# The first key and value panels of layer b as a pair in seven products, and one adding transfer cut in halves

## The chip, the cores and the metric

The kernel runs on one core of a Trainium2 chip. The metric is the device time of one execution in microseconds. The engines have these names in the profile: PE (TensorE, matrix products), PEld (its weight loads), DVE (VectorE), ACT (ScalarE), POOL (GpSimd), SP (SyncE, which here only issues transfers).

## The reference, cut to what matters

256 tokens of width 2048 pass a two-layer trunk. Everything is float32.

```python
def sq_relu_mlp(h, g, w1, w2):
    a = jax.nn.relu(rms_norm(h, g) @ w1)          # w1: 2048 x 8192
    return (a * a) @ w2                            # w2: 8192 x 2048
...
    # layer a
    q, k, v, fz = split(rms_norm(h, a_norm_g) @ a_w_in)      # 2048 x (3 * 2048 + 16)
    h = h + forgetting_attention(q, k, v, logf) @ a_w_out
    h = h + sq_relu_mlp(h, ...)
    # keys and values, once, from the stream after layer a
    kv = rms_norm(h, kv_norm_g) @ kv_w                       # 2048 x 4096
    k_sh, v_sh = split(kv)
    # layer b
    q = rms_norm((rms_norm(h, b_norm_g) @ b_w_q), b_q_g)     # 2048 x 2048
    h = h + chunked_relbias_attention(q, k_sh, v_sh, b_rel) @ b_w_out
    h = h + sq_relu_mlp(h, ...)
```

All weights are read once; nearly all the work is the products of 256 tokens with these matrices.

## The kernel before, in words

**Arithmetic.** A float32 product is made of three fast ones. Each weight tile is split into `hi` (ACT, line 318, a rounded copy) and `lo` (DVE, line 319, the rest); each activation tile is split alike. `passes` (lines 585, 587, 589) then gives hi*hi, hi*lo and lo*hi into one PSUM bank.

**Units.** Weights come in units of 128 x 1024 floats (`UN`, 512 KB). A plain unit holds two tiles of 128 rows for one panel of 512 output columns, and `products` makes 12 matrix products of 128 x 128 x 512 of it: two row tiles, two blocks of 128 tokens, three passes. A panel needs 8 plain units.

**Pairs.** Two panels side by side can share their first rows as a `Pair`. Its two token blocks, its even and odd row tiles, and its two panels form a 2 x 2 times 2 x 2 block product, done in seven products in place of eight. The seven right-hand operands are the *forms* `11 T3 T2 T1 21 T4 22`, of the four weight blocks 11, 12, 21, 22: T3 = 22 + 12, T2 = T3 + 11, T1 = 12 + 11, T4 = T2 + 21. An ordinary pair takes two couples of row tiles so (its forms are 1024 wide, 6 matrix products each, in `form_products`), and leaves 6 plain units of each panel (a2 to a7, b2 to b7). A deep pair, in the MLPs, takes four couples (forms 2048 wide, issued as two halves, f and h). Some left-hand operands are sums and differences of activations, made beforehand by `sums` (tiles named S, Sh).

**Who adds.** T3 and T2 are made on DVE (`make`, line 951). T1 and T4 are made by a transfer that adds in flight: `put` (line 960) issues it on POOL's queue, straight from the weights in memory onto the tile of 12 (for T1) or of T2 (for T4). The four blocks are loaded by `bring` (line 925, SP's queue), plain units by `load` (line 294, SP's queue). T2's tile may be overwritten with T4 only when T2 has been split, so `issue` calls `put` for T4 right behind the split of T2's last half:

```python
        if form and form.pair.deep and form.name == "T3":
            make(form.pair, "T2", int(half))
        elif form and half == form.pair.wide:
            ...
            elif form.name == "T2" and form.pair.adds:
                put(form.pair, "T4")
```

**Order.** The whole order of units and forms is a list made before anything is emitted (`plan_heads`, `plan_mlp`, `plan_out`). The last three plain units of a pair (b5, b6, b7) go between the first forms of the next, so every two products of six are followed by one of twelve. `fetch` and `top_up` keep two or three units split ahead of PE, and three more loaded ahead of that. Each engine runs its instructions in the written order. What surrounds the products (norms, transposes, softmax, activation splits) is cut into steps and put into `fill`; `run_fill` emits the next slot after each product. `TABLES` says in which slot each step goes, and, for each pair, how many plain units before its start its blocks 12, 22, 21, 11 are brought and its T3 and T1 are made.

**Transposes by transfer.** Hidden activations are turned by `hop` (line 459): 16 small transfers, alternately on POOL's and SP's queue, named q<-z.

**Around the change.** In layer b, after layer a's MLP, two pairs of query panels (orders "query" and "") are made of `xb`. Then come the keys and values, of `xkv`: the first key panel with its 8 plain units and the first value panel with 5 (`panels`, from `heads_b`), its last three going between the forms of the pair of the second key and value panel; three pairs follow, then two pairs of the output projection, then MLP b. The query pairs end with their own b5, b6, b7, one behind the other. In both MLPs the first block of w1 is an ordinary pair ("early"); the second, with index 1, is the first deep one, of order "ahead1"; later ones alternate "ahead0" and "ahead1" with w2's ("deep0", "deep1").

Of the kernel before, what the change touches and what calls it, by code (L numbers as in the profile page):

```python
# [9 lines left out]
F32 = mybir.dt.float32  # L10
F32R = mybir.dt.float32r
AF = mybir.ActivationFunctionType
ALU = mybir.AluOpType
AX = mybir.AxisListType

P = 128
# [3 lines left out]
KT = D // P  # L20
H = 16
# [6 lines left out]
UN = 1024  # L28
AHEAD = 2
TABLES = {  # L30
    "ATA": ((11, 13, 15, 19, 9), (9, 12, 16, 18, 11), (8, 13, 15, 19, 9), (9, 9, 12, 12, 10)),
    "ATB": ((10, 13, 14, 18, 9), (9, 13, 15, 17, 11), (9, 12, 15, 17, 10), (7, 10, 12, 12, 9)),
# [13 lines left out]
    "LONG": ((0, 1, 2, 5, 9, 10, 11, 14, 14), (0, 0, 0, 4, 7, 9), (1, 0, 1, 2, 5, 5), (1, 0, 1, 4, 5, 5)),  # L46
    "OFH": (11, 10, 1, 7, 7, 7),
    "OFK": (10, 9, 4, 9, 8, 4),
# [3 lines left out]
    "OSH": (7, 9, 7, 5, 5, 1),  # L52
    "OSK": (9, 7, 4, 7, 5, 1),
    "OUTH": "F a2 a3 b2 a4 a5 b3 b4 F G F G b5 a6 a7 G b6 b7 G c2 G c3 G d2 c4 c5 G c6 c7 d3 d4",
    "OUTK": "a2 a3 F b2 a4 F b3 a5 F b4 b5 G G a6 a7 G b6 G c2 b7 d2 G c3 G c4 c5 c6 G c7 d3 d4",
    "QF": (4, 4, 2, 3, 2, 1),
    "QS": (10, 4, 4, 8, 3, 1),
    "RI": (3, 5, 7, 5),
    "SHORT": ((4, 0, 0, 3, 6, 8, 8, 9, 12), (2, 2, 3, 3, 7, 7, 8, 10, 13), (2, 0, 0, 2, 6, 7), (0, 0, 0, 2, 4, 5)),
# [13 lines left out]
    "XOH": (9, 12, 13, 11),  # L73
    "XOK": (9, 14, 12, 14),
    "XS": (0, 5, 6, 2),
}
EARLY = 3
LAZY = ("qkv", "kv", "out0", "out1")
UA = UN // 512
REL = 384  # L80
WIDE = UN + 512
DEEP = 2 * UN
# [16 lines left out]
def trunk(ctx: ExitStack, tc: tile.TileContext, xT, xr, gs, hg, bf, wgate, w_in, w_oa, w1a, w1fa, w1sa, w2fa, w2sa,  # L99
# [48 lines left out]
    units = deque()  # L148
# [45 lines left out]
    def plan_mlp(w1, w1f, w1s, w2f, w2s, rest, when, more=None):  # L194
# [18 lines left out]
        for m, (second, c, q) in enumerate(seq):  # L213
            i = 2 * c + q
            if second:
                add(None, w2f, w2s, i, WIDE2, "deep%d" % q, TABLES["W2L" if i == 7 else "W2S" if q else "W2F"], DEEP)
            else:
                add(w1, w1f, w1s, i, WIDE1, "ahead%d" % q if i else "early", TABLES["W1E" + when] if not i else TABLES["W1I" + when] if i == 1 else TABLES["W1S" if q else "W1F"], DEEP)
            pairs[-1].at = second, c, q
# [4 lines left out]
        plan, rest = join(pairs, rooms, rest)  # L224
        return queue(plan + rest)

# [32 lines left out]

    def plan_heads(w, when, w_out):  # L260
        pairs = []
        for j in range(1, w.shape[0] // 16):
            src = [[w[16 * j + 8 * q + u] for u in range(8)] for q in range(2)]
            big = {k: src[int(k[1]) - 1][int(k[0]) - 1] for k in ("11", "12", "21", "22")}
            pairs.append(Pair(big, src, "qkv" if when == "H" else "kv", j % 2 == 1, TABLES[when + ("F" if j == 1 else "S")]))
            pairs[-1].at = 2 * j
        tail = Tail(w, 8)
        units.extend(w[i] for i in range(13))
        plan, rest = join(pairs, {"12": "k0", "22": "k1", "11": "v0", "21": "v1"}, [(tail, 0, u) for u in range(KT // UA - 3, KT // UA)])
        q = pairs[-1].rooms  # L270
        more, rest = plan_out(w_out, {"12": q["11"], "22": q["12"], "11": q["21"], "21": q["22"]}, rest, when)
        return queue(plan + more), rest, tail

    plan_h, rest, tail_h = plan_heads(w_in, "H", w_oa)
    plan_a = plan_mlp(w1a, w1fa, w1sa, w2fa, w2sa, rest, "H", w_qb)
    plan_k, rest, tail_k = plan_heads(w_kv, "K", w_ob)
    plan_b = plan_mlp(w1b, w1fb, w1sb, w2fb, w2sb, rest, "K")
    ready = deque()

# [20 lines left out]
    def issue(parts=1):  # L300
# [20 lines left out]
        if form and form.pair.deep and form.name == "T3":  # L321
            make(form.pair, "T2", int(half))
        elif form and half == form.pair.wide:
            if form.name == "T3":
                make(form.pair, "T2")
            elif form.name == "T2" and form.pair.adds:
                put(form.pair, "T4")
# [373 lines left out]
    class Rooms:  # L701
# [3 lines left out]
        def open(self):  # L705
            self.t = prob.tile([P, 4 * UN], F32, name="pbuf", tag="p", bufs=1)
            self.n = dict.fromkeys(self.at, 0)

        def __call__(self, name):
            first, n = self.at[name]  # L710
            i = first + self.n[name] % n
            self.n[name] += 1
            return self.t[:, i * 3 * P : (i + 1) * 3 * P]
# [196 lines left out]
    def bring(p, name):  # L910
        if p.order == "out1":
            i = int(name in ("11", "21"))
            if i not in p.box:
                p.box[i] = acts.tile([P, DEEP], F32, name="wB", tag="act")
            p.t[name] = p.box[i][:, name[0] == "2" and UN or 0 :][:, :UN]
        elif p.order in LAZY:
            f, n = owner.get(p.rooms[name], (None, None))
            assert f is None or {"12": "T1", "21": "21", "11": "11", "22": "22"}[n] in f.issued, ("room busy", name, n)
            assert n != "11" or "T2" in f.has
            owner[p.rooms[name]] = p, name  # L920
            p.t[name] = sub(p.rooms[name])[:, UN:]
        else:
            p.t[name] = room(p.rooms[name], "w" + name)
        p.has.add(name)
        SY.dma_start(p.t[name][:, : p.cols], p.big[name])

    def make(p, name, half=None):
# [3 lines left out]
        elif name == "T3":  # L931
            if p.order in ("query", ""):
                t[name] = query_room(0)
            elif p.order in LAZY:
                t[name] = acts.tile([P, 2 * UN], F32, name="wT3", tag="act")[:, :UN]
# [16 lines left out]

    def put(p, name):

# [4 lines left out]
        p.has.add(name)  # L959
        G.dma_start(p.t[name][:, : p.cols], p.big[other], accum_op=ALU.add)  # L960

# [55 lines left out]
    def mlp(plan, x, Sx, st, last, more=None):  # L1017
# [58 lines left out]

        run(plan, open_pair)

# [143 lines left out]
    def heads_b(out):  # L1222
# [19 lines left out]
        evacs = [f(g) for g in range(NG) for f in (of_k, of_v)]  # L1242
        box = [13]

        def after():
            prepare(plan_k[0][0], box[0])
            box[0] -= 1

        panels(xkv, evacs[:1], None, after)
        panels(xkv, evacs[1:2], None, after, tail=tail_k)  # L1250
        base = turns[0]

        last = next(p for p, q, i in plan_k[::-1] if isinstance(p, Pair) and p.order in LAZY[:2])
# [104 lines left out]
```

## Time and profile before

| | |
|---|---|
| time, median of 3 runs | 2059.22 us (2059.14 to 2059.76) |
| time of the profiled execution | 2062.13 us |
| its span, first to last instruction | 2060.3 us |
| PE busy | 2047.3 us, 9068 matrix products |
| DVE busy | 1778.3 us (86%) |
| ACT busy | 1400.0 us (68%) |
| share of the 16 transfer engines, software queue | 22.4% |
| share of the 16 transfer engines, SP's queue | 63.9% |
| granted PE clock, mean | 0.999 |

The profile page gives one execution. Rows of the timeline read: start in us, length in us, engine, line, operation, out<-in, count, and in brackets how long the engine sat idle before it and what ended that. The end of a matrix product is modelled, and products overlap in the pipeline, so lengths of rows overlap; the time that PE needs is read from one start to the next. Rows of waits read: who waited for whom, microseconds in total, times, longest.

### The profile page before, as it was taken

Reading aid. Unit: us, or ns where it says so; the run is one execution under the profiler, and the core shown is the slowest. Engines: PE = TensorE matmul, PEld = TensorE weight load, DVE = VectorE, ACT = ScalarE, POOL = GpSimd, SP = SyncE. Lnnn points to the kernel's source line nnn. Section 1 sums busy time; section 2 is a strip of 40 time slices with the busy share of each in tenths; the row PEclk is TensorE's granted clock in tenths of the full one; section 3 lists DMA queues with packets and bytes.
Section 4 is the critical chain, followed back from the end, with each engine's and each line's share of the span. In section 5 each row is a group of like instructions: output and inputs, shape, how many; then the busy total and the mean of one; then the engine's idle time right before and its main releaser. Section 6 shows DMA issues by size and latency. Waiting matters only on the chain.

```text
span 2060.3 us, 27092 instructions
## 1 busy us (share of the span) xinstructions
PE 2047.3 (99%) x9068; PEld 1690.6 (82%) x9068; DVE 1778.3 (86%) x2058; ACT 1400.0 (68%) x1799; POOL 238.7 (12%) x347
## 2 busy tenths in 40 slices
PE   9999999999999999999999999999999999999999
PEld 8888888878888888888888888888788887888887
DVE  7788798899898899899987778888988988988996
ACT  7766566677677677677788566666766675776764
POOL 1121010011111102101012111001111111111020
PEclk9999999999999999999999999999999999999999
DMA  8898897898888898898878988889988888888985
GB/s 330 258 301 252 275 278 249 292 274 266 293 255 287 267 295 272 248 290 276 252 247 273 288 265 269 251 256 295 279 288 269 266 267 277 262 285 258 293 263 150
DMA packets 174444, 556.72 MB, mean 270 GB/s; under 512 B 40528, under 2 KB 69088, under 8 KB 151264
## 3 DMA queue, kind: packets, MB, share of 16 engines
q1 hardware_dynamic: 153824, 464.99, 63.9%
q0 software_dynamic: 20192, 89.70, 22.4%
q8 instruction: 71, 1.16, 0.2%
q14 instruction: 69, 0.57, 0.1%
q10 hardware_dynamic: 288, 0.30, 0.1%
HBM read 515.02 MB, written 27.29 MB: 263 GB/s over the span
## 4 chain that ended last, share of the span: by engine, by line
PE 88%; DMA 4%; issue 3%; DVE 3%; ACT 1%; SPq 0%; POOL 0%; ACTq 0%; DVEq 0%; POOLq 0%
PE acc L589 21%; PE acc L585 21%; PE acc L587 21%; PE s L585 8%; PE s L587 8%; PE s L589 8%; DVE lo L319 1%; DMA wT<-in_w1fb 1%; DMA q<-turn 1%; PE po L720 1%; PE po L757 1%; DMA w<-in_w2fb 1%; ACT hi L318 1%; DVE z L433 0%; DMA turn<-z 0%
## 5 line engine op out<-in xcount | busy, mean ns | idle before, releaser
L319 DVE TENSOR_TENSOR lo<-raw,hi 128x1024 fp32r<-128x1024 f32 (+1 forms) x414 | 500.3, 1213 | 81.0 <-ACT hi L318 76.6
L318 ACT ACTIVATE hi<-raw 128x1024 fp32r<-128x1024 f32 (+1 forms) x414 | 435.1, 1055 | 195.2 <-PE acc L587 128.6
L585 PE MATMUL acc<-hi,act 128*128 128x512 f32 x1784 | 500.5, 393 | 4.3 <-ACT hi L318 3.7
L589 PE MATMUL acc<-lo,act 128*128 128x512 f32 x1784 | 493.9, 390 | 0.2
L587 PE MATMUL acc<-hi,act 128*128 128x512 f32 x1784 | 493.8, 390 | 0.1
L585 PEld LDWEIGHTS acc<-hi,act 128*128 128x128 f32 x1784 | 333.1, 188 | 75.3 <-ACT hi L318 6.1
L587 PEld LDWEIGHTS acc<-hi,act 128*128 128x128 f32 x1784 | 335.1, 188 | 71.6 <-DVE act L414 1.0
L589 PEld LDWEIGHTS acc<-lo,act 128*128 128x128 f32 x1784 | 334.5, 188 | 72.4 <-DVE lo L319 3.1
L318 ACT ACTIVATE hi<-w 128x1024 fp32r<-128x1024 f32 x258 | 271.4, 1059 | 125.9 <-PE acc L587 83.5
L319 DVE TENSOR_TENSOR lo<-w,hi 128x1024 fp32r<-128x1024 f32 x258 | 310.6, 1219 | 19.6 <-ACT hi L318 17.7
L319 DVE TENSOR_TENSOR lo<-wT,hi 128x1024 fp32r<-128x1024 f32 x220 | 266.9, 1222 | 68.6 <-ACT hi L318 64.7
L318 ACT ACTIVATE hi<-wT 128x1024 fp32r<-128x1024 f32 x220 | 231.8, 1060 | 103.7 <-PE acc L587 42.2
L585 PE MATMUL s<-hi,act 128*128 128x512 f32 x530 | 146.3, 391 | 0.0
L589 PE MATMUL s<-lo,act 128*128 128x512 f32 x530 | 145.0, 389 | 0.4 <-DVE lo L319 0.4
L587 PE MATMUL s<-hi,act 128*128 128x512 f32 x530 | 144.7, 388 | 0.0
L459 POOL DMA_DIRECT2D q<-z x192 | 95.7, 511 | 250.9 <-DVE z L433 214.4
L589 PEld LDWEIGHTS s<-lo,act 128*128 128x128 f32 x530 | 99.2, 188 | 21.4 <-DVE lo L319 1.1
L587 PEld LDWEIGHTS s<-hi,act 128*128 128x128 f32 x530 | 99.4, 188 | 20.6
L585 PEld LDWEIGHTS s<-hi,act 128*128 128x128 f32 x530 | 99.2, 188 | 20.4
L585 PE MATMUL s<-hi,S 128*128 128x512 f32 x288 | 89.6, 392 | 0.0
L587 PE MATMUL s<-hi,S 128*128 128x512 f32 x288 | 88.7, 389 | 0.0
L589 PE MATMUL s<-lo,S 128*128 128x512 f32 x288 | 88.6, 389 | 0.0
(213 smaller groups left out, 2236.3 us busy)
## 6 DMA issues: line engine op xcount, KB each, us to landing
raw<-in_w_in SPq DMA_DIRECT2D x75, 512.0 KB, 5.8
w<-in_w2fa SPq DMA_DIRECT2D x32, 1024.0 KB, 6.2
w<-in_w2fb SPq DMA_DIRECT2D x32, 1024.0 KB, 6.6
w<-in_w1fa SPq DMA_DIRECT2D x28, 1024.0 KB, 7.4
w<-in_w1fb SPq DMA_DIRECT2D x28, 1024.0 KB, 7.1
raw<-in_w2sa SPq DMA_DIRECT2D x52, 512.0 KB, 7.1
raw<-in_w_kv SPq DMA_DIRECT2D x52, 512.0 KB, 5.4
raw<-in_w2sb SPq DMA_DIRECT2D x51, 512.0 KB, 7.6
```

The source lines that it names most:

```text
L318: S.activation(hi[:, c], raw[:, c], AF.Copy)
L319: V.tensor_tensor(lo[:, c], raw[:, c], hi[:, c].bitcast(F32), op=ALU.subtract)
L459: (G if i % 2 else SY).dma_start(dst[32 * j : 32 * j + 32, i * n : (i + 1) * n], z[32 * i : 32 * i + 32, j * n : (j + 1) * n])
L585: TE.matmul(ps[:, cols], xh, cut(hi, j), start=first, stop=False, **kw)
L587: TE.matmul(ps[:, cols], xl, cut(hi, j), start=False, stop=False, **kw)
L589: TE.matmul(ps[:, cols], xh, cut(lo, j), start=False, stop=last, **kw)
L720: TE.matmul(s[:, P : 3 * P], q[:, a, P:T], k[:, a], start=True, stop=True)
L757: TE.matmul(po[:, :T], v[:, 0, a * P : (a + 1) * P], pT[:, :2], start=True, stop=False)
```

## The change

1. The first key and value panels of layer b become an ordinary pair too (order "kv0", table "KZ"): 12 plain units and 7 forms in place of 16 plain units. The calls of `panels` in `heads_b` go. The weights are laid out for it on the host, for all of w_kv.
2. The three last units of the second query pair no longer stand alone at the end of layer a's plan; they go between the first forms of the new pair, and `run` for that plan prepares the new pair's blocks ahead (its argument `follow`).
3. Rooms: the second query pair takes lower halves of the tiles whose upper halves hold the new pair's blocks; the new pair's T3 takes the last quarter of the tile `query`; the softmax tile `pbuf`, which shares a place with `query`, is allotted at its first use and not at the start.
4. In both MLPs the block of w1 with index 1 has order "second" in place of "ahead1" (same list of products). For it, T4's adding transfer is issued in two halves: the left one behind the split of T2's first half, the right one behind that of its second half.
5. Nearly all slots and distances in `TABLES` that belong to the projections, the output projections, the attention and the start of the MLPs are others. Those of the later MLP blocks stay (`T`, `W1F`, `W1S`, `W2F`, `W2S`; `W2L` has one other number).

```diff
-    "KX": ((7, 7, 8, 11, 11), (13, 15), (15, 17), (18, 20)),
+    "KX": ((7, 7, 8, 11, 11), (12, 13), (17, 18), (19, 20)),
+    "KZ": (7, 8, 3, 7, 5, 3),
...
+        "kv": "a2 F a3 a4 F a5 a6 a7 F b2 b3 b4", "qkv": "a2 a3 a4 F a5 F a6 b2 a7 F b3 b4", "kv0": "a2 F a3 a4 F a5 a6 a7 F b2 b3 b4",
...
-    "T0H": ((0, -1, 6, 6, 7, 7, 7, 10, 11), (1, -1, 5, 7, 7, 7, 8, 9, 9), (1, 4, 6, 6, 7, 7), (0, -1, 4, 4, 4, 5)),
-    "T0K": ((0, -1, 5, 5, 6, 6, 6, 7, 10), (1, -1, 5, 5, 6, 6, 7, 8, 8), (1, 3, 6, 7, 7, 7), (0, -1, 4, 4, 4, 4)),
-    "W1EH": (12, 13, 2, 15, 7, 6),
-    "W1EK": (14, 14, 9, 12, 11, 5),
+    "T0H": ((1, -1, 6, 6, 6, 6, 6, 8, 8), (0, -1, 4, 5, 6, 6, 7, 8, 8), (0, 4, 6, 7, 7, 7), (1, -1, 5, 5, 5, 5)),
+    "T0K": ((1, -1, 5, 5, 6, 6, 6, 7, 10), (1, -1, 5, 5, 6, 6, 7, 8, 8), (1, 3, 6, 7, 7, 7), (0, -1, 4, 4, 4, 4)),
+    "W1EH": (14, 15, 2, 10, 7, 6),
+    "W1EK": (13, 14, 7, 12, 12, 4),
     "W1F": (7, 5, 1, 5, 4, 3),
-    "W1IH": (11, 7, 6, 9, 4, 1),
-    "W1IK": (11, 7, 3, 9, 4, 3),
+    "W1IH": (10, 7, 6, 8, 4, 2),
+    "W1IK": (10, 7, 3, 9, 4, 1),
...
-                add(w1, w1f, w1s, i, WIDE1, "ahead%d" % q if i else "early", ...
+                add(w1, w1f, w1s, i, WIDE1, ("second" if i == 1 else "ahead%d" % q) if i else "early", ...
...
-        return queue(plan + rest)
+        return (queue(plan), rest) if more is not None else (queue(plan + rest), [])
...
+        elif form and form.pair.order == "second" and form.name == "T2":
+            put(form.pair, "T4", int(half))
         elif form and half == form.pair.wide:
...
         def open(self):
-            self.t = prob.tile([P, 4 * UN], F32, name="pbuf", tag="p", bufs=1)
+            self.t = None
...
+        elif p.order == "":
+            p.t[name] = sub(p.rooms[name])[:, :UN]
...
+            elif p.order == "kv0":
+                t[name] = query_room(3)
...
-    def put(p, name):
+    def put(p, name, half=None):
...
-        G.dma_start(p.t[name][:, : p.cols], p.big[other], accum_op=ALU.add)
+        cols = slice(0, p.cols) if half is None else slice(half * UN, half * UN + UN)
+        G.dma_start(p.t[name][:, cols], p.big[other][:, cols], accum_op=ALU.add)
...
-        run(plan, open_pair)
+        run(plan, open_pair, None, plan_k[0][0] if more else None)
...
-        panels(xkv, evacs[:1], None, after)
-        panels(xkv, evacs[1:2], None, after, tail=tail_k)
```

More of the change, by code (lines that the diff above doesn't have):

```diff
@@ L30 @@
 TABLES = {
-    "ATA": ((11, 13, 15, 19, 9), (9, 12, 16, 18, 11), (8, 13, 15, 19, 9), (9, 9, 12, 12, 10)),
-    "ATB": ((10, 13, 14, 18, 9), (9, 13, 15, 17, 11), (9, 12, 15, 17, 10), (7, 10, 12, 12, 9)),
[1 row of a table removed]
+    "ATA": ((10, 13, 15, 19, 9), (9, 12, 15, 18, 12), (8, 13, 15, 19, 9), (9, 9, 12, 12, 10)),
+    "ATB": ((11, 12, 14, 18, 9), (9, 13, 15, 17, 11), (9, 12, 15, 17, 10), (7, 10, 12, 12, 10)),
[1 row of a table added]
     "GS": (1,),
[11 rows of a table removed]
-    "LONG": ((0, 1, 2, 5, 9, 10, 11, 14, 14), (0, 0, 0, 4, 7, 9), (1, 0, 1, 2, 5, 5), (1, 0, 1, 4, 5, 5)),
-    "OFH": (11, 10, 1, 7, 7, 7),
-    "OFK": (10, 9, 4, 9, 8, 4),
[3 rows of a table removed]
-    "OSH": (7, 9, 7, 5, 5, 1),
[12 rows of a table added]
+    "LONG": ((0, 1, 2, 5, 9, 10, 11, 14, 14), (0, 0, 0, 4, 7, 9), (0, 0, 1, 2, 5, 5), (1, 0, 1, 4, 5, 5)),
+    "OFH": (11, 10, 2, 7, 7, 6),
+    "OFK": (9, 9, 4, 8, 8, 4),
[3 rows of a table added]
+    "OSH": (10, 7, 9, 6, 5, 1),
     "OSK": (9, 7, 4, 7, 5, 1),
[L54 to L57, printed above, removed]
+    "OUTH": "F a2 a3 a4 b2 a5 b3 b4 F F G G b5 a6 a7 G b6 b7 G c2 G c3 G d2 c4 c5 c6 G c7 d3 d4",
+    "OUTK": "a2 a3 F b2 a4 F b3 a5 F b4 b5 G G a6 a7 G b6 G c2 b7 G d2 c3 G c4 c5 c6 G c7 d3 d4",
+    "QF": (4, 3, 2, 4, 2, 1),
+    "QS": (10, 4, 4, 8, 4, 2),
     "RI": (3, 5, 7, 5),
-    "SHORT": ((4, 0, 0, 3, 6, 8, 8, 9, 12), (2, 2, 3, 3, 7, 7, 8, 10, 13), (2, 0, 0, 2, 6, 7), (0, 0, 0, 2, 4, 5)),
[1 row of a table removed]
+    "SHORT": ((4, 0, 0, 4, 7, 7, 7, 8, 11), (2, 2, 3, 3, 7, 7, 8, 11, 13), (4, 0, 0, 2, 6, 6), (0, 0, 1, 2, 4, 5)),
[1 row of a table added]
     "T": ((1, -1, 5, 14, 14, 14, 15, 20, 20), (0, 2, 8, 10, 10, 14, 18, 20, 22), (0, -1, 5, 6, 7, 7), (0, -1, 4, 5, 5, 5)),
[4 rows of a table removed]
[4 rows of a table added]
     "W1F": (7, 5, 1, 5, 4, 3),
[2 rows of a table removed]
[2 rows of a table added]
     "W1S": (8, 6, 4, 5, 4, 1),
     "W2F": (6, 5, 1, 5, 4, 3),
[1 row of a table removed]
[1 row of a table added]
     "W2S": (7, 7, 4, 5, 3, 1),
-    "XOH": (9, 12, 13, 11),
-    "XOK": (9, 14, 12, 14),
-    "XS": (0, 5, 6, 2),
+    "XOH": (9, 13, 12, 11),
+    "XOK": (10, 14, 12, 14),
+    "XS": (0, 5, 5, 0),
 }
 EARLY = 3
-LAZY = ("qkv", "kv", "out0", "out1")
+LAZY = ("qkv", "kv", "kv0", "out0", "out1")
 UA = UN // 512
@@ L217, in plan_mlp @@
             else:
-                add(w1, w1f, w1s, i, WIDE1, "ahead%d" % q if i else "early", TABLES["W1E" + when] if not i else TABLES["W1I" + when] if i == 1 else TABLES["W1S" if q else "W1F"], DEEP)
+                add(w1, w1f, w1s, i, WIDE1, ("second" if i == 1 else "ahead%d" % q) if i else "early", TABLES["W1E" + when] if not i else TABLES["W1I" + when] if i == 1 else TABLES["W1S" if q else "W1F"], DEEP)
             pairs[-1].at = second, c, q
@@ L258, in plan_out, with plan_heads @@
         return plan, [(b, 1, u) for u in (5, 6, 7)]
-    def plan_heads(w, when, w_out):
+    def plan_heads(w, when, w_out, rest=None):
         pairs = []
-        for j in range(1, w.shape[0] // 16):
+        for j in range(1 if rest is None else 0, w.shape[0] // 16):
             src = [[w[16 * j + 8 * q + u] for u in range(8)] for q in range(2)]
             big = {k: src[int(k[1]) - 1][int(k[0]) - 1] for k in ("11", "12", "21", "22")}
-            pairs.append(Pair(big, src, "qkv" if when == "H" else "kv", j % 2 == 1, TABLES[when + ("F" if j == 1 else "S")]))
+            order = "qkv" if when == "H" else "kv" if j else "kv0"
+            pairs.append(Pair(big, src, order, j % 2 == 1, TABLES["KZ" if j == 0 else when + ("F" if j == 1 else "S")]))
             pairs[-1].at = 2 * j
-        tail = Tail(w, 8)
-        units.extend(w[i] for i in range(13))
-        plan, rest = join(pairs, {"12": "k0", "22": "k1", "11": "v0", "21": "v1"}, [(tail, 0, u) for u in range(KT // UA - 3, KT // UA)])
+        tail = None
+        if rest is None:
+            tail = Tail(w, 8)
+            units.extend(w[i] for i in range(13))
+            rest = [(tail, 0, u) for u in range(KT // UA - 3, KT // UA)]
+        plan, rest = join(pairs, {"12": "k0", "22": "k1", "11": "v0", "21": "v1"}, rest)
         q = pairs[-1].rooms
@@ L274, in trunk @@
     plan_h, rest, tail_h = plan_heads(w_in, "H", w_oa)
-    plan_a = plan_mlp(w1a, w1fa, w1sa, w2fa, w2sa, rest, "H", w_qb)
-    plan_k, rest, tail_k = plan_heads(w_kv, "K", w_ob)
-    plan_b = plan_mlp(w1b, w1fb, w1sb, w2fb, w2sb, rest, "K")
+    plan_a, rest = plan_mlp(w1a, w1fa, w1sa, w2fa, w2sa, rest, "H", w_qb)
+    plan_k, rest, _ = plan_heads(w_kv, "K", w_ob, rest)
+    plan_b, rest = plan_mlp(w1b, w1fb, w1sb, w2fb, w2sb, rest, "K")
     ready = deque()
@@ L705, in open @@
         def open(self):
-            self.t = prob.tile([P, 4 * UN], F32, name="pbuf", tag="p", bufs=1)
+            self.t = None
             self.n = dict.fromkeys(self.at, 0)
         def __call__(self, name):
+            if self.t is None:
+                self.t = prob.tile([P, 4 * UN], F32, name="pbuf", tag="p", bufs=1)
             first, n = self.at[name]
@@ L1242, in heads_b @@
         evacs = [f(g) for g in range(NG) for f in (of_k, of_v)]
[L1243 to L1247, printed above, removed]
-        panels(xkv, evacs[:1], None, after)
-        panels(xkv, evacs[1:2], None, after, tail=tail_k)
         base = turns[0]
@@ L1335 @@
         "w2sa": m2[0][2],
-        "w_kv": np.concatenate([_cols_a(kv[:, :1024]), _cols_a(kv[:, 1024:], True)]),
+        "w_kv": _cols_a(kv, True),
         "w_qb": _cols_a(i["b_w_q"][0], True),
```

31 rows, old and new, of the table TABLES are left out of this document.

## The prediction

> **What bounds the kernel now.** I read the page first, then the waits, then PE's own timeline for the places where its products do not follow one another without a gap.
>
> ```profile
> span 2060.3 us, 27092 instructions
> PE 2047.3 (99%) x9068; PEld 1690.6 (82%) x9068; DVE 1778.3 (86%) x2058; ACT 1400.0 (68%) x1799; POOL 238.7 (12%) x347
> ```
>
> PE is busy for 2047.3 of 2060.3 us. So an edit can help in two ways only: fewer matrix products, or fewer of the few microseconds in which PE stands or runs slowly. The change tries both. Where PE stands is told by the waits (who, for whom: us, times, longest) and by PE's timeline around the block of w1 with index 1, in layer a and in layer b:
>
> ```profile
> ACT hi L318 <- DMA wT<-in_w1fb: 12.8, 7, 3.8
> ACT hi L318 <- DMA wT<-in_w1fa: 8.6, 4, 3.2
> ```
>
> ```profile
> 433.36 0.61 PE L589 MATMUL acc<-lo,act 128*128 128x512 f32 x2
> 435.20 0.73 PE L585 MATMUL acc<-hi,act 128*128 128x512 f32 x2 [1.23 <-ACT hi L318]
> 437.95 0.62 PE L589 MATMUL acc<-lo,act 128*128 128x512 f32 x2
> 438.41 1.08 PE L585 MATMUL acc<-hi,act 128*128 128x512 f32 x4
> ...
> 1453.16 0.73 PE L589 MATMUL acc<-lo,act 128*128 128x512 f32 x2
> 1455.61 1.09 PE L585 MATMUL acc<-hi,act 128*128 128x512 f32 x2 [1.71 <-ACT hi L318]
> 1459.59 0.62 PE L589 MATMUL acc<-lo,act 128*128 128x512 f32 x2
> 1460.06 1.08 PE L585 MATMUL acc<-hi,act 128*128 128x512 f32 x4
> ```
>
> What a product costs is read from plain units (x4 per pass, three passes) and from forms (x2 per pass), at the old panels' start and at the first form behind them:
>
> ```profile
> 1118.19 1.07 PE L585 MATMUL acc<-hi,act 128*128 128x512 f32 x4
> 1120.91 1.07 PE L585 MATMUL acc<-hi,act 128*128 128x512 f32 x4
> ...
> 1153.55 0.61 PE L585 MATMUL s<-hi,act 128*128 128x512 f32 x2
> 1154.91 1.07 PE L585 MATMUL acc<-hi,act 128*128 128x512 f32 x4
> ```
>
> A plain unit takes 1120.91 - 1118.19 = 2.72 us, a form of six 1154.91 - 1153.55 = 1.36 us, a pass of two 0.45 us.
>
> **Part 1: seven products in place of eight.** Sixteen plain units took 16 x 2.72 = 43.52 us of PE; 12 units and 7 forms take 12 x 2.72 + 7 x 1.36 = 42.16 us. That is 6 products of 9068, **1.36 us** less, and it lies wholly on the path, since PE is the path. The stretch has no gap to win besides:
>
> ```profile
> 1030.00:1050.00 20.00, 19.59 (x87) 15.91 (x86) 18.45 (x20) 16.11 (x26) 1.13 (x2) 1.00 0.84 271
> ...
> 1090.00:1110.00 20.00, 20.00 (x90) 16.57 (x89) 14.23 (x16) 17.38 (x31) 3.08 (x2) 1.00 0.73 218
> 1110.00:1130.00 20.00, 20.00 (x90) 16.53 (x89) 14.57 (x17) 14.30 (x25) 5.34 (x6) 1.00 0.94 294
> 1130.00:1150.00 20.00, 20.00 (x90) 16.57 (x89) 13.28 (x15) 12.62 (x23) 3.61 (x3) 1.00 1.00 337
> ```
>
> The columns are the stretch, its length, then busy us of PE, PEld, DVE, ACT, POOL, then granted clock, share of the transfer engines, GB/s. What the pair adds beside PE comes from these groups (busy us, mean ns):
>
> ```profile
> L319 DVE TENSOR_TENSOR lo<-raw,hi 128x1024 fp32r<-128x1024 f32 (+1 forms) x414 | 500.3, 1213 | 81.0 <-ACT hi L318 76.6
> L318 ACT ACTIVATE hi<-raw 128x1024 fp32r<-128x1024 f32 (+1 forms) x414 | 435.1, 1055 | 195.2 <-PE acc L587 128.6
> L951 DVE TENSOR_TENSOR wT<-wT,w 128x1024 f32<-128x1024 f32 x62 | 76.0, 1225 | 2.1
> L990 DVE SCALAR_TENSOR_TENSOR acc<-s,p 128x512 f32<-128x512 f32 x24 | 16.6, 692 | 0.9 <-PE s L589 0.9
> L985 ACT ACTIVATE p<-s 128x512 f32<-128x512 f32 x24 | 14.4, 598 | 31.4 <-PE s L589 31.4
> ```
>
> DVE gets three more splits, T3 and T2, and two combinations of accumulators: 3 x 1.21 + 2 x 1.23 + 2 x 0.69 = 7.5 us. ACT gets three splits and three copies of an accumulator: 3 x 1.06 + 3 x 0.60 = 5.0 us. The pair starts where the query pair's b5 started, near 1110, and lasts with those three units 42.16 + 8.16 = 50 us. In 1110 to 1150 DVE has 40 - 27.85 = 12.2 us free and ACT 40 - 26.92 = 13.1 us, so both fit on the whole, and DVE would come to nearly 18 of 20. Locally it is tighter: between the first forms two units need 2 x 1.06 us of ACT in 4.08 us of PE instead of 1.06 in 2.72. The nearest stretch that did stall, 1030 to 1050, had DVE at 18.45 and ACT at 16.11 of 20 and lost 0.41 us of PE. Bounds: nothing, or several such losses, 2 us; below nothing it cannot go, as 1090 to 1150 has no idle PE. I take **+0.6**, by that row.
>
> T1 and T4 of the new pair are two more issues on POOL, and 1 MB more on the software queue. Adding transfers of this size in the other key and value pairs show:
>
> ```profile
> L960 POOL DMA_DIRECT2D R<-in_w_kv x3: 853/860/902, 1148.9 to 1226.6; - x3
> DMA to landing us min/median/max: 5.3/6.3/9.1
> ```
>
> T4 has, from T2's product to its own, b7, T1, a2, 21, a3, a4: 4 x 2.72 + 2 x 1.36 = 13.6 us against 9.1 at worst; T1 has three plain units and then 11, b5, T3, b6, T2, b7, over 20 us, less the two or three units that splitting runs ahead. Both are covered; were they not, the stall would be the excess. POOL is busy for 3 to 5 of 20 us there; the query norms' small operations queued behind a `put` that waits for DVE stand there too; ACT scales by their result, and the cover is the two or three split units ahead of PE, 5 to 8 us. The blocks' loads on SP come about 15 us earlier than the units they replace, where the transfer engines have room (0.73 against 1.00 later).
>
> **Part 2: T4 in halves.** The 1 MB adding transfer is issued when T2's second half is split; the tile is due when T4's product comes up.
>
> ```profile
> 418.57 2.55 DVE L319 TENSOR_TENSOR lo<-wT,hi 128x1024 fp32r<-128x1024 f32 x2
> ...
> 1438.32 2.54 DVE L319 TENSOR_TENSOR lo<-wT,hi 128x1024 fp32r<-128x1024 f32 x2
> ```
>
> ```profile
> 421.69 0.93 POOL L960 DMA_DIRECT2D wT<-in_w1fa  x1 [3.74 <-DVE lo L319]
> ...
> 1441.43 0.95 POOL L960 DMA_DIRECT2D wT<-in_w1fb  x1 [2.72 <-DVE lo L319]
> 1446.74 3.47 POOL L459 DMA_DIRECT2D q<-z  x7 [4.37 <-DVE z L433]
> ```
>
> ```profile
> 434.09 2.01 ACT L318 ACTIVATE hi<-wT 128x1024 fp32r<-128x1024 f32 x2 [2.34 <-DMA wT<-in_w1fa]
> ...
> 1454.50 2.00 ACT L318 ACTIVATE hi<-wT 128x1024 fp32r<-128x1024 f32 x2 [1.85 <-DMA wT<-in_w1fb]
> ```
>
> In layer b it takes until ACT's start about 13.1 us (1441.43 to 1454.50), in layer a 12.4 (421.69 to 434.09), and in both ACT, then PE, wait for it. The loss in layer a: PE was due at 433.36 + 0.45 = 433.81 and starts at 435.20, 1.39 us; the two halves of T4 then take until 438.41, 3.21 us in place of 2 x 1.36 = 2.72. Together 1.9. In layer b: due 1453.61, starts 1455.61, 2.0 us; the two halves last until 1460.06, 4.45 in place of 2.72, 1.7 more. Together 3.7. The 1.7 are the clock:
>
> ```profile
> 1455.60:1459.30 3.70, 3.69 (x9) 2.95 (x10) 3.70 (x4) 2.91 (x3) 0.00 (x0) 0.54 0.85 322
> ```
>
> The granted clock (0.54) is lost for 3.7 us right behind the stall: 3.7 x 0.46 = 1.7. Not every stall of that length does it; a later one, in w2, runs at 0.45 us a pass straight afterwards:
>
> ```profile
> 1733.90 1.07 PE L589 MATMUL s<-lo,act 128*128 128x512 f32 x4
> 1736.90 0.70 PE L585 MATMUL acc<-hi,Sh 128*128 128x512 f32 x2 [1.93 <-DVE acc L990]
> 1737.43 0.62 PE L587 MATMUL acc<-hi,Sh 128*128 128x512 f32 x2
> ```
>
> The Trainium skill, "TensorE: Matmul & The Clock Gate", section Part 1, puts the drop behind an idle window of about 3.4 us of a free-running monitor, so by its rule this stall would cost only its own 2.0 us and part 2 could win 1.7 less; the row of granted clock decides here, since a stall of 2.0 us was followed by it.
>
> With halves, the left one can go once T2's first half is split, about 1.3 us earlier (half of the x2 rows: 1439.6 in b, 419.8 in a). If the transfer as a whole does not end any sooner, the right half still lands at 434.1 and 1454.5, but it is due one form, 1.36 us, later, and the left half is long there. The right half's hi is then done 1.06 us after its landing: 435.15 against 435.17 due in a, 1455.5 against 1454.97 due in b; its lo, 1.22 us later, is due two passes, 0.91 us, after hi. Left over: 0.3 in a, 0.9 in b. So part 2 wins 5.6 at most, if the right half comes earlier too, and 5.6 - 1.2 = 4.4 if it doesn't, and I take the middle, **5.0**. In b the drop of the clock goes with the stall. The added issue (0.95 us on POOL) stands ahead of q<-z's part on POOL, which begins 4 us later, and so delays nothing. Next late after it is nothing of T4; the next gap of PE is the one at 1736.90, which this edit does not touch.
>
> **Part 3: the other slots.** The products of layer a, and their count, stay; only the steps beside them move. PE's gaps there that a slot can move are, beside those above, of half a microsecond each; I take 0, and 2 us either way.
>
> **Sum.** On the profiled execution: -1.36 + 0.6 - 5.0 = -5.8, so 2062.13 - 5.8 = 2056.3, and a span near 2054.5. That execution is 2.91 us above the median of the timed runs. Whatever the timed runs do not have of it may be in these very stalls, so I let a third of the 2.91 off the gain: 4.8 us, and 2059.22 - 4.8 = **2054.4**.
>
> **Rivals.**
>
> *The halves arrive too late.* Two transfers of 512 KB could go one after the other, each with its own start and landing. At the median and the maximum of the rows of that size: left half 1439.6 + 6.3 = 1445.9, right half 1445.9 + 9.1 = 1455.0, which in a is 419.8 + 15.4 = 435.2. Then T4's second half is 1.1 and 1.1 late in hi, 1.4 with lo, and in b the clock is lost again (1.7): 4.5 of the 5.6 remain. Time 2059.22 - 1.36 - 1.1 + 0.6 = 2057.4. For it: the same 16 engines serve SP's loads, and the whole transfer needs up to 13 us though its median is less:
>
> ```profile
> DMA to landing us min/median/max: 8.0/10.5/13.0
> ```
>
> Against it: halves overlap, and 6.3 is far below 10.5. The Trainium skill, "DMA: Bandwidth & Descriptors", section Bandwidth, speaks for it: batch to 1 MiB and more, as each transfer has a fixed cost of about 2.0 us; by that the right half would land 2 us later. If the splits wait for both halves, so that the change does not do what it says, the time is the same. Chance 0.2.
>
> *The stalls were mostly the profiled execution's.* If the timed runs lack all 2.91 us of them, part 2 wins 2.1: 2059.22 - 1.36 - 2.1 + 0.6 = 2056.4. For it: the gap between the two times. Against: the transfer's lateness repeats in both layers. Chance 0.2.
>
> *Slower: ACT becomes the bound where the new pair starts.* ACT has 17.38 of 20 us busy in 1090 to 1110, of which splitting weights is
>
> ```profile
> 1090.00:1110.00 20.00, 7.84 (x8) 1.00 0.73 218
> ```
>
> so 9.5 us are other steps, mostly the activations of the keys and values, and these move into slots 17 to 20, towards the new forms. Four forms and three units last 13.6 us and need 7 x 1.06 = 7.4 of ACT; 6.2 are left. If all 9.5 fall there, 3.3 us are late, with a drop of the clock 5.0; it decides against the gain as soon as the lateness is over 5 us, for instance when it meets the query norms' wait behind POOL twice (2 x 5.0 = 10.0 with clock): 2059.22 + 10.0 - 1.36 - 4.0 = 2063.9. Against it: in 1110 to 1130 ACT has 5.7 us free. Chance 0.1.
>
> **How the numbers follow.** The forecast has 0.5. About 0.2%, 4.1 us here, is what a measurement of this kernel can tell from no change; faster by more is below 2055.1. My forecast lies 0.7 below that line. Of its 0.5, 0.43 falls below, and of the second rival's 0.2, which lies 1.3 above the line, 0.07 (part 3 can move either by 2 us): faster 0.5. Slower, above 2063.3, has the third rival: 0.1. Same has the first rival and what is left of the others: 0.4. The range goes from 2059.22 - 1.36 - 5.6 - 2 = 2050.3 (every stall of part 2, and part 3's 2 us) to 2059.22 - 1.36 + 0.6 + 2 = 2060.5 (nothing of part 2, and part 3 against it). Outside are the rest of the third rival, and half of the cases beyond either end, 2 in 10.
>
> **What would show it.** In the changed profile: 9062 products; two issues of wT<-in_w1fa and wT<-in_w1fb about 1.3 us apart for index 1, ACT no longer idle on them, no wait of PE there, granted clock 1.00 behind it; 7 forms and 12 units where the panels were, PE at 20.00 of 20 in the stretches from 1090 to 1160, DVE near 18. I am wrong if PE waits for hi or lo in that stretch, if the right half of T4 lands over 1.4 us later than the whole did, or if gaps of PE come up in layer a.

## The result, and the profile after

The changed kernel takes 2055.39 us (median of 14 runs, 2053.08 to 2059.78); the kernel before, on the same chip, 2059.18 us (14 runs, 2056.45 to 2061.5). The ratio is 0.998, 95% interval 0.9973 to 0.9987, so 2.7 to 5.6 us less. The profiled execution took 2053.61 us. Its page, where it answers to the lines shown of before:

```profile
span 2051.8 us, 27095 instructions
PE 2042.6 (100%) x9062; PEld 1688.9 (82%) x9062; DVE 1784.1 (87%) x2065; ACT 1404.8 (68%) x1805; POOL 244.2 (12%) x351
```

The two profiled spans differ by 8.5 us, the medians by 3.8: executions of one kernel differ by several microseconds, among other things because a transfer lands a little sooner or later in front of a wait (layer b's T4 below). So I don't compare spans below. Outside the new pair and a few units of the output projections, PE makes the same products in the same order in the kernels of this table, so a stretch of its work is timed from the start of one product to the start of another (numbered as in the kernel before), and a difference is thereby put in its place. Later runs are in this table too; their edits follow. "T4 whole" and "T4 in halves" say how T4's transfer is issued for the w1 block with index 1.

```
us of PE between two products, one execution each (us = start in the kernel before)
                  T4 whole                                               T4 in halves
stretch     us    before before_2 b_slots_a a_pair a_whole a_s5whole | b_halves after after_2 a_late a_t0h a_slot5 a_best
1620- 1900  364   64.45  63.50    64.09     64.91  66.72   63.54     | 63.48    63.47 64.97   63.50  65.83 63.72   64.41
1900- 2600  428  161.81 161.73   162.42    161.79 161.83  161.01     |161.95   161.31 161.51 161.05 161.25 160.07 161.81
4640- 4760 1054   26.99  26.99    26.99     27.17  27.45   27.46     | 27.25    28.17 27.95   28.16  27.95 28.10   26.99
4760- 5080 1081   72.53  72.53    72.53     71.17  71.17   71.89     | 72.53    71.17 71.17   71.17  71.17 71.17   71.17
6260- 6450 1414   47.30  43.94    45.19     44.58  46.09   44.19     | 43.65    43.65 43.89   43.65  43.65 43.69   43.67
7000- 7800 1586  183.53 181.37   181.35    181.35 181.36  183.69     |181.36   181.37 181.93  181.36 181.35 182.45 181.39
8500- 9067 1928  128.16 128.33   128.29    127.38 127.37  127.37     |128.23   127.36 127.37  127.37 127.37 127.38 127.36
```

4760-5080 holds the first key and value panels; 6260-6450 holds T4 of layer b's w1 block with index 1; 1900-2600 that of layer a; 4640-4760 the query pairs. Names that begin with b are the kernel before with an edit, with a the changed kernel with one; the new pair is in the a-kernels and in after. Below, PE's *excess* at a place is what PE loses there against its even pace of 0.227 us a product, gaps over 0.2 us counted.

**Layer b's T4.** PE's, POOL's and ACT's timelines of the changed kernel, at the place where PE stood for 2.0 us and then ran at half clock:

```profile
1450.13 0.61 PE L594 MATMUL acc<-hi,act 128*128 128x512 f32 x2
1450.65 0.74 PE L596 MATMUL acc<-lo,act 128*128 128x512 f32 x2
1451.23 0.64 PE L592 MATMUL acc<-hi,act 128*128 128x512 f32 x2
...
1452.39 0.73 PE L596 MATMUL acc<-lo,act 128*128 128x512 f32 x2
...
1454.34 1.07 PE L592 MATMUL acc<-hi,act 128*128 128x512 f32 x4
```

```profile
1436.48 0.92 POOL L974 DMA_DIRECT2D wT<-in_w1fb  x1 [1.80 <-issue]
1438.66 0.86 POOL L974 DMA_DIRECT2D wT<-in_w1fb  x1 [1.26 <-DVE lo L324]
```

```profile
1448.83 1.30 ACT L402 ACTIVATE Sh<-sum 128x512 fp32r<-128x512 f32 x2 [1.51 <-DVE sum L396]
1450.04 1.99 ACT L323 ACTIVATE hi<-wT 128x1024 fp32r<-128x1024 f32 x2
```

```profile
1455.00:1460.00 5.00, 5.00 (x23) 4.13 (x22) 5.00 (x6) 3.77 (x5) 0.00 (x0) 1.00 0.99 406
```

Two issues, 2.2 us apart. ACT goes from its Sh step straight to T4's two halves and waits for no transfer, passes follow at 0.45 to 0.7 us, and the granted clock is 1.00 (the last row; columns as in the prediction's rows of this kind).

**Layer a's T4.** Here PE stands as long as before, but for another engine:

```profile
431.83 0.61 PE L594 MATMUL acc<-hi,act 128*128 128x512 f32 x2
433.80 0.72 PE L596 MATMUL acc<-lo,act 128*128 128x512 f32 x2 [1.35 <-DVE lo L324]
```

```profile
430.74 1.04 ACT L323 ACTIVATE hi<-wT 128x1024 fp32r<-128x1024 f32 x1
432.13 1.06 ACT L323 ACTIVATE hi<-wT 128x1024 fp32r<-128x1024 f32 x1 [0.35 <-DMA wT<-in_w1fa]
```

```profile
429.92 1.23 DVE L1048 TENSOR_TENSOR act<-q,act 128x1024 fp32r<-128x1024 f32 x1 [1.91 <-ACT q L1044]
431.06 0.42 DVE L395 TENSOR_TENSOR sum<-q 128x256 f32<-128x256 f32 x1
...
432.53 1.22 DVE L324 TENSOR_TENSOR lo<-w,hi 128x1024 fp32r<-128x1024 f32 x1
```

T4 is there in time (the ACT rows). But DVE stood 1.91 us for ACT's step of the first hidden block, then made that block's low part and its sums, and only at 432.53 the lo that PE wanted from 432.28. It is the lo of the block in front of T4 (w, not wT), wanted one pass before T4. It is done at 433.75, and PE goes on at 433.80.

**The queries.** The one place that became slower. The waits around T3 of the second query pair:

```profile
DVE query L964 <- DMA R<-in_w_qb: 2.6, 1, 2.6
```

```profile
PE s L596 <- DVE lo L324: 0.7, 1, 0.7
```

DVE stands 2.6 us for a block that was asked for only then, and a split behind it reaches PE late.

**The new pair itself.** The stretches, columns as before:

```profile
1090.00:1110.00 20.00, 20.00 (x90) 16.57 (x89) 16.52 (x18) 17.53 (x33) 6.51 (x4) 1.00 1.04 330
1110.00:1130.00 20.00, 20.00 (x90) 16.53 (x89) 17.75 (x21) 16.58 (x26) 5.74 (x5) 1.00 1.00 303
1130.00:1150.00 20.00, 20.00 (x90) 16.57 (x89) 12.59 (x14) 12.00 (x22) 3.60 (x3) 1.00 0.90 264
```

PE stays at 20.00 of 20; in 1110 to 1130 DVE rises from 14.57 to 17.75 and ACT from 14.30 to 16.58, under what the stretch holds.

### The profile page after: what moved, and what is told of

It is laid out like the page before. It is cut to its first block, busy times and chain, and to the rows that moved or that the text cites. A ratio compares the mean times of both kernels' runs of the same rounds, so it can differ in the third digit from the quotient of the medians.

```text
span 2051.8 us, 27095 instructions
## 1 busy us (share of the span) xinstructions
PE 2042.6 (100%) x9062; PEld 1688.9 (82%) x9062; DVE 1784.1 (87%) x2065; ACT 1404.8 (68%) x1805; POOL 244.2 (12%) x351
## 4 chain that ended last, share of the span: by engine, by line
PE 94%; DVE 3%; DMA 1%; ACT 1%; issue 1%; SPq 0%; ACTq 0%; POOL 0%; DVEq 0%; POOLq 0%
PE acc L596 22%; PE acc L592 22%; PE acc L594 22%; PE s L596 9%; PE s L592 9%; PE s L594 9%; DVE lo L324 1%; DMA raw<-in_w_in 1%; PE po L729 1%; PE po L766 1%; ACT hi L323 0%; PE po L767 0%; PE po L728 0%; DMA turn<-z 0%; DMA raw<-in_w_qb 0%
## 5 line engine op out<-in xcount | busy, mean ns | idle before, releaser
L324 DVE TENSOR_TENSOR lo<-raw,hi 128x1024 fp32r<-128x1024 f32 (+1 forms) x409 | 494.1, 1212 | 80.4 <-ACT hi L323 76.3
L323 ACT ACTIVATE hi<-raw 128x1024 fp32r<-128x1024 f32 (+1 forms) x409 | 429.7, 1054 | 192.2 <-PE acc L594 131.0
L323 ACT ACTIVATE hi<-w 128x1024 fp32r<-128x1024 f32 x254 | 267.1, 1058 | 127.9 <-PE acc L594 85.2
L324 DVE TENSOR_TENSOR lo<-w,hi 128x1024 fp32r<-128x1024 f32 x254 | 305.5, 1218 | 15.3 <-ACT hi L323 13.5
```

The lines of the kernel that those rows point to most:

```text
L323: S.activation(hi[:, c], raw[:, c], AF.Copy)
L324: V.tensor_tensor(lo[:, c], raw[:, c], hi[:, c].bitcast(F32), op=ALU.subtract)
```

## The experiments

The main theory is called late transfer: the gain beside the 1.36 us of the pair is that T4 no longer comes after its product is due. The rival is that the moved slots give it.

**Halves alone** (b_halves), on the kernel before (cut: the block with index 1 also takes the order "second", and `put` its argument `half`, as in the change):

```diff
+        elif form and form.pair.order == "second" and form.name == "T2":
+            put(form.pair, "T4", int(half))
```

> The kernel before with one edit: T4 of the w1 block with index 1 in halves; no new pair, all slots as before. Theory 'late transfer' (T4's 1 MB comes after its product is due, halves cure that): in layer b the stall at T4 and the clock's drop behind it go, 3.0 to 3.7 us of the profiled span; in layer a 1.6 to 1.9 us; over many runs 2 to 5 us below before (ratio 0.9976 to 0.999). Theory 'other slots' (the gain of the whole change comes from the steps that moved, in layer a and at the queries): within 1 us of before, and ACT still waits on wT. PE products 9068.

Measured: ratio 0.9998, interval 0.9987 to 1.0008, so 2.7 us less to 1.6 us more. Layer b's stretch was 43.65 us, as short as in any kernel, as expected; layer a's 161.95 us, no gain. PE waits near 433 all the same (its waits between 425 and 440: sum, count, longest in us):

```profile
PE acc L591 <- DVE lo L319: 1.6, 1, 1.6
```

That lo is T4's own. DVE made it behind the first hidden block's work, as it did in the kernel before, where the wait for the transfer covered it; DVE's timeline of the kernel before:

```profile
432.58 1.22 DVE L1034 TENSOR_TENSOR act<-q,act 128x1024 fp32r<-128x1024 f32 x1
433.71 0.42 DVE L388 TENSOR_TENSOR sum<-q 128x256 f32<-128x256 f32 x1
...
435.19 2.36 DVE L319 TENSOR_TENSOR lo<-wT,hi 128x1024 fp32r<-128x1024 f32 x2
```

The right half of T4 was late besides, as ACT's timeline of b_halves shows:

```profile
435.69 1.06 ACT L318 ACTIVATE hi<-wT 128x1024 fp32r<-128x1024 f32 x1 [2.58 <-DMA wT<-in_w1fa]
```

Its hi is done at 436.75, 1.5 us after the 435.28 at which PE would have wanted it. The forecast of 2 to 5 us is not borne out over the runs.

**The change without halves** (a_whole): the same two lines taken out of the changed kernel.

> The changed kernel with T4 of index 1 whole again; the new pair and its slots stay. 'Late transfer': PE waits for hi of wT in layer b again, 1.5 to 2.2 us, with or without a drop of the clock of 1.7 us, and in layer a about 1.4 us, partly hidden there by the other stall that the changed kernel has at that place; time 1 to 4 us above the changed kernel, that is within 2 us of before. 'Other slots': as the changed kernel, 2055.4, ratio 0.998. PE products 9062.

Measured: 2058.42 us, ratio 0.9983 (0.9973 to 0.9992). Layer b's stretch is 46.09 us, with 1.8 us of excess. The wait for T4's hi is back, but it is 0.7 of the 1.8; 0.9 is a wait one pass earlier, for the lo of the block in front of T4. Most of the gain over before is there without halves: 3.5 us by the ratio, of 5.4 in a_late (next), on the same chip.

**Both halves written behind T2's second half** (a_late):

```diff
-            put(form.pair, "T4", int(half))
+            if half:
+                put(form.pair, "T4", 0)
+                put(form.pair, "T4", 1)
```

> The changed kernel, with both halves of T4 issued one behind the other after the split of T2's second half, so cut in two but not earlier. If the later due time of the right half is what helps: at most 0.6 us more stall per layer than the changed kernel, time within 1 us of it. If the earlier issue of the left half helps (1.3 to 2.2 us earlier): the left half lands late, PE waits 1 us or more for its hi in layer b, with the clock dropping up to 1.7 more, time 1 to 3 us above the changed kernel.

Measured: 2055.69 us, ratio 0.9974 (0.9963 to 0.9984), layer b's stretch 43.65 us. On the same chip the mean of its 7 runs is 2.6 us below that of a_whole's 11 (interval by resampling the runs, 1.1 to 4.1), so with the pair and its slots halves do gain time. It does not tell the two cases apart, since the issues stand where they stood:

```profile
1436.53 0.92 POOL L976 DMA_DIRECT2D wT<-in_w1fb  x1 [1.52 <-issue]
1438.71 0.86 POOL L976 DMA_DIRECT2D wT<-in_w1fb  x1 [1.25 <-DVE lo L324]
```

In the changed kernel they are at 1436.48 and 1438.66. POOL is idle there and goes as soon as the left half's own split is done, wherever the issue is written. So this is the changed kernel once more.

The transfer's packets say more on the two cases in layer b. Counted from the time at which T4's product was due by PE's even pace, the whole transfer's last packet came 0.2 to 1.5 us ahead in the six executions with T4 whole. In the seven with halves the right half's last packet came 0.5 to 1.8 us ahead and the left half's 4.3 to 5.8. So the whole hardly ends sooner in halves. ACT begins on the left half 1.0 us ahead of due, over 3 us after its last packet, and its issue is earlier by 1.8 to 2.2 us only, so the left half does not need that. This points to the due times: the left half is long there, and the right half is due a form later. A run with the issue alone moved was not made; b_due below moves the due time alone.

**The slots of layer a alone** (b_slots_a): the kernel before with the changed kernel's tables for layer a.

> The kernel before, with the changed kernel's table entries for layer a alone (its projections, attention, output projection and MLP start: ATA, HF, HM, HS, OFH, OSH, OUTH, SHORT, T0H, W1EH, W1IH, XOH, XS); no new pair, T4 whole. Theory 'slots of layer a' (the moved steps there are worth the microseconds that halves alone did not give): 1.5 to 3 us below before, ratio near 0.9988. Theory 'pair and its slots': within 1 us of before.

Measured: 2058.81 us, ratio 0.9994 (0.9985 to 1.0004): 1.2 us less, not clear of none.

**The pair and layer b's slots alone** (a_pair): the changed kernel with layer a's tables of before and T4 whole.

> The changed kernel with T4 of index 1 whole and the table entries of layer a as before: what is left of the change is the new pair and the slots of layer b. By the count of products alone 1.36 us below before, ratio 0.9993. Theory 'pair and its slots': 3 us or more below before, ratio at or under 0.9985. Theory 'slots of layer a': 1 to 2 us below.

Measured: 2058.0 us, ratio 0.9984 (0.9975 to 0.9993): 3.3 us less, more than the products' 1.36. The key and value stretch is 71.17 instead of 72.53 us, 1.36 to the digit. The last stretch is 127.38 instead of 128.13 to 128.33 in the kernel before and all its variants; the difference lies wholly at T4 of the last w1 block, where ACT waits 1.5 us for the transfer in a_pair (none in the changed kernel) and PE not at all, against ACT's 3.8 us before:

```profile
ACT hi L318 <- DMA wT<-in_w1fb: 3.8, 1, 3.8
```

So 0.9 us come from the slots at the end of layer b. Of the tables for these last blocks only one number of `W2L` differs (block 21 is brought one unit earlier), so it is the likely entry; it was not tried alone.

**The kernel before once more** (before_2):

> The kernel before once more, for its profile. If the stalls at T4 belong to the kernel: PE waits 1.3 us or more near 433 and near 1453 again. If they belonged to one execution: at most one of the two shows. The 2.1 us near 1735 should not return, if it was an accident of that execution.

Measured: 2056.07 us, 6.06 less than its first profiled execution, with the same program. Near 433 PE's excess is 1.6 us again. In layer b the wait is nearly gone in this execution, and the 2.1 us near 1735 are gone too (181.37):

```profile
ACT hi L318 <- DMA wT<-in_w1fb: 0.2, 1, 0.2
```

So T4's lateness in layer b belongs to the kernel, but its size to the execution: 43.94 to 47.30 us in six executions with T4 whole, mean 45.21, against 43.65 to 43.89 in seven with halves, mean 43.69. Halves are worth 1.5 us there (1.4 without a_whole's 0.9 us for another block), not the 3.7 of the one profile; among the profiles the drop of the clock occurs in that one alone.

**Later due, T4 whole** (b_due), on the kernel before (cut: the block with index 1 also takes the order "second"):

```diff
-        "second": "a4 F F a5 a6 a7 F b4"},
+        "second": "a4 F a5 F a6 a7 F b4"},
```

> The kernel before with T4 whole, but in the w1 block with index 1 the product with T4 comes one plain unit (2.72 us) later: list a4 F a5 F a6 a7 F b4 in place of a4 F F a5 a6 a7 F b4. Theory 'late by its due time': in layer b the T4 stretch falls to 43.7 to 44.0 us, as with halves, from 43.9 to 47.3 with T4 whole (mean of five 45.2); time 0.5 to 3 us below before. Rival (another wait takes its place): the stretch stays at 44.5 or more.

Measured: layer b's stretch 43.89 us, as expected; but the time is 2063.82 us, ratio 1.0006 (0.9993 to 1.0018). The next stretch (6450-7000) takes 127.57 instead of about 125.04, with waits for lo like this:

```profile
1472.71 1.20 PE L589 MATMUL s<-lo,act 128*128 128x512 f32 x4 [0.76 <-DVE lo L319]
```

The wait for the transfer goes with the later due time alone, and waits for lo come in its place; what makes these late was not followed.

**Layer a's slots, first try** (a_t0h): `T0H[0]` from `(1, -1, 6, 6, 6, 6, 6, 8, 8)` to `(1, -1, 6, 6, 7, 7, 7, 10, 11)`.

> The changed kernel with one table entry of layer a other: the steps of the first hidden block of MLP a after its transpose in slots 6 6 7 7 7 10 11, as before, in place of 6 6 6 6 6 8 8. Theory: the 1.5 us in which PE waits for a lo near 433 come from three ACT steps and a DVE step of that block set into one slot ahead of a unit's split; then that stall goes and layer a wins 1.2 to 1.8 us against the changed kernel, time about 2054. Rival (the right half of T4 is what is late in layer a, and takes the stall's place): PE still waits 1 us or more there, for hi of wT.

Measured: 2057.02 us, ratio 0.9977 (0.9969 to 0.9985). PE's excess near 433 stays at 1.7 us, for lo and not for hi: T4's own lo, made at 437.42 behind the hidden block's sums, as in b_halves. My slots were wrong, and so was the rival.

**Second try** (a_slot5): `T0H[0] = (1, -1, 5, 5, 6, 6, 6, 7, 10)`, as layer b has it.

> The changed kernel with the steps of MLP a's first hidden block in slots 5 5 6 6 6 7 10, those that layer b has, in place of 6 6 6 6 6 8 8. Theory: layer a's 1.5 us wait near 433 comes from that block's DVE steps standing in front of a split, since its transpose is used one slot later than in layer b; then the wait falls to 0.3 or less, as in layer b, and the time is 1.0 to 1.8 us below the changed kernel, ratio to before 0.997 to 0.9975. Rival (the transpose lands too late for slot 5): ACT then waits for q<-z ahead of the splits, and PE's wait stays at 1.5 us or grows.

Measured: 2056.67 us, ratio 0.9979 (0.997 to 0.9988). The excess near 433 is 0.23 us, the stretch 160.07, the shortest of all; the gain in time is below what the runs can tell.

**The same with T4 whole** (a_s5whole):

> The changed kernel with the slots 5 5 6 6 6 7 10 in layer a, and T4 whole. Theory 'two covers in layer a' (the late transfer and the hidden block's steps each make PE wait there, and taking away one leaves the other): PE waits 1 us or more again near 433, now for hi of wT, and the stretch is 161.3 to 161.9 us, against 160.1 with both cures. Rival (the slots alone were the cause): it stays near 160.1. In layer b the T4 stretch is 44 us or more.

Measured: 2059.12 us (one execution). PE waits again, 1.5 us of excess, for hi:

```profile
PE acc L590 <- ACT hi L323: 1.1, 1, 1.1
```

So either cure alone leaves 1.5 to 1.8 us near 433, and both leave 0.2 (a_slot5) to 0.7 (a_best): two late things at one place, each of which covers the other. The whole stretch bears it out less well: 161.01, under the 161.3 expected.

**The changed kernel once more** (after_2):

> The changed kernel once more, for its profile: layer b's T4 stretch 43.65 us within 0.1, the key and value stretch 71.17, the query stretch about 28.1, the last stretch 127.4, layer a's T4 stretch 161.1 to 161.4. What differs from the first profile by more than 0.3 us lies elsewhere, mostly before 1060 us.

Measured: 2056.43 us; the stretches as expected but for layer b's T4 (43.89, 0.24 over 43.65) and layer a's (161.51, 0.1 over the range). What it has over its first profile lies in 1620-1900 (1.5 us) and 4500-4640 (0.85), and 7000-7800 (0.56).

**Both repairs** (a_best): a_slot5 and

```diff
-    "QS": (10, 4, 4, 8, 4, 2),
+    "QS": (10, 4, 4, 8, 3, 2),
```

> The changed kernel with two table edits: the slots 5 5 6 6 6 7 10 for MLP a's first hidden block, and T3 of the second query pair made 3 plain units before its start in place of 4 (its block 22 is brought 4 before). Theory 'DVE stands for a load' (T3's addition is queued 2.6 us for the landing of the block brought in the same slot, and a split behind it comes late at PE): the query stretch, 28.1 us in four profiles of the changed slots with halves, falls to 27.0 to 27.2 as before, and layer a's T4 stretch stays near 160.1 against 161.3; together 1.5 to 2.3 us below the changed kernel, ratio to before 0.9968 to 0.9975. Rival (DVE is simply full there, 19.9 of 20 us): the stretch stays at 27.9 or more.

Measured: 2054.68 us, ratio 0.9967 (0.9955 to 0.998), the lowest of all, though its interval overlaps the changed kernel's. The query stretch is 26.99 us, exactly as before, with DVE as full as ever, so fullness was not it:

```profile
1070.00:1090.00 20.00, 20.00 (x90) 16.57 (x89) 19.76 (x25) 18.02 (x31) 5.61 (x4) 1.00 0.72 207
```

DVE's waits there, in the same kernel:

```profile
DVE query L964 <- DMA R<-in_w_qb: 1.2, 1, 1.2
```

DVE's wait for the block fell from 2.6 to 1.2 us, and PE's to none. Layer a's stretch was 161.81 this time, so that repair's gain isn't shown by it.

## Why the prediction was right

The time, 2055.39, lies within the range and 1.0 above the forecast of 2054.4; the gain was 3.8 and not 4.8 us. But the terms of the sum did not come out as written, and that they came out so near together is in part luck: part 2 was far too large, and part 3, put at nothing, made up for some of it.

- *Part 1, 1.36 us*: exact, 72.53 to 71.17 us in all but one execution with the pair.
- *Part 1, +0.6 for DVE and ACT*: within its bounds of nothing to 2 us but nearly twice the size (1.0 to 1.2 us in the changed kernel's executions), and wrong in place and cause, so luck. Neither DVE nor ACT was too full in the new pair. T3 of the second query pair was put into the slot that brings its block, and DVE stood for the load. I had read that table entry as one more moved step of no weight; the row to look at was T3's own wait in the kernel before (`DVE query L951 <- DMA w<-in_w_qb: 1.0, 1, 1.0`), which left no room.
- *Part 2, -5.0*: the mechanism holds in layer b, the size was off by a factor of more than three. Layer b gives 1.5 us on the mean of executions, not 3.7, since the profiled execution was one with an unusually late transfer and the only one with the drop of the clock. That is the second rival, and I had let only a third of 2.91 us off for it. Layer a gives nothing by halves alone. "Next late after it is nothing of T4" was wrong: next late was T4's own lo, two passes behind its hi, which DVE made after its work on the hidden block; the wait for the transfer hid it. DVE's rows of the kernel before, shown under b_halves, had it. In the changed kernel, with its slots, the lo of the block in front of T4 comes late in its place.
- *Part 3, 0*: about -1.4. The end of layer b gives 0.9; in layer a the stretch 1900-2600 gives about 0.5 (161.81, 161.73 to 161.31, 161.51, 161.05 in a_late). This 0.5 belongs to the slots and the halves together: it shows neither with the slots alone (162.42 in b_slots_a, 161.83 in a_whole) nor with halves alone (161.95).
- *Sum by the stretches*: -1.36 + 1.1 - 1.5 - 0.9 - 0.5 = -3.2, against -3.8 measured, interval -2.7 to -5.6.
- *The signs*: the two issues stood 2.2 us apart and not 1.3, and one sign of being wrong came: PE's gap near 433 in layer a stayed, for lo.
- *First rival, halves too late*: not in layer b. In b_halves' layer a ACT stood 2.6 us for the right half, whose hi was 1.5 us late, so it can be; there PE lost nothing by it, as lo held it up longer. *Slower rival*: PE does not wait in 1105 to 1160 in the changed kernel, and ACT had room.
- *The skill's rules*: 1 MiB as the least size of a transfer spoke against halves ("DMA: Bandwidth & Descriptors" in the Trainium skill, section Bandwidth), and layer b's stretch disagrees: 43.69 against 45.21. The rule of the clock gate ("TensorE: Matmul & The Clock Gate" in the Trainium skill, section Part 1) would have kept the drop out, and left 1.7 us less for part 2, nearer to the runs.

## What to carry to other kernels

Where PE is the bound, time its work product by product in several executions before pricing a stall: a count of products comes out to the digit, a stall on a transfer can be several times as long in one execution as in the next (0.3 to 3.7 us for layer b's T4). When a wait is taken away, look at each operand of the same form and of the block in front of it, not only at the latest one: a second one may be late by nearly as much. And don't ask for a block in the same step that computes with it on an engine that works in order.

## What was not expected of the hardware

While products ran, the granted clock fell to half for 3.4 us in one of 14 profiled executions, behind a stall of 1.9 to 2.0 us. Stalls of 1.9 us (a_t0h, near 404), 2.1 us (w2, the kernel before), 2.2 us (a_s5whole) and 2.8 us (a_whole, near 403) were not followed by it; what decides is open. The drops are hardly confined to that one execution: the mean granted clock on record is 0.998 or 0.999 in 17 of the 73 timed runs of the kernel before beside the experiments, while the fall behind the last product, at the end of every profile, takes it to 0.9995 at the least. Where it fell in them, and whether T4 had a part in it, the record does not tell.

The 1 MB adding transfer of layer b in the kernel before, issued at 1441.43, moved its first packet of 8 KB at 1446.0; until then SP's packets took 0.92 of the engines' time. Its 128 packets of 8 KB took 0.63 us each; the halves' 256 packets of 4 KB, in the changed kernel, 0.33 us each (medians).
